# Scores of differential attention on the two row halves of the array

## The chip, the core and the metric

One NeuronCore of a Trainium2 chip runs the kernel. Its engines are TensorE (matrix products; its weight loads are a row of their own in the profile), VectorE, ScalarE, GpSimd, and SyncE, which issues the transfers. The metric is the device time of one execution in microseconds (us).

## The reference

One step of a streaming encoder with one layer: a prompt of 2048 frames of width 1024, and eight running streams that add 16 frames each to a past of 2048. Two attention branches run side by side (four differential heads, four latent-attention heads, MLA), each is gated, projected, and their gated sum is projected and added to the input. The change concerns the differential heads over the prompt:

```python
def diff_attention(q1, q2, q_pos, k1, k2, v, k_pos, lam):
    mask = chunk_mask(q_pos, k_pos)
    s1 = jnp.einsum('bqhd,bkhd->bhqk', q1, k1).astype(jnp.float32) * DIFF_SCALE
    s2 = jnp.einsum('bqhd,bkhd->bhqk', q2, k2).astype(jnp.float32) * DIFF_SCALE
    attn = masked_softmax(s1, mask) - lam * masked_softmax(s2, mask)
    return jnp.einsum('bhqk,bkhd->bqhd', attn.astype(v.dtype), v)
```

Queries and keys of either map ("lane") have 64 dimensions. The mask lets a query see keys up to the end of its own chunk of 64. Inputs and results are float32.

## The kernel before

Products run in a rounded float32 form that TensorE takes in one pass (F32R). To keep the accuracy of float32, an operand is split into a high part and a low part, and a product becomes several: high x high, high x low, low x high.

The kernel has stages: projections of the input (`_phase_a`), the latent heads' queries, keys and values (`_phase_a2`), the prompt's attention (`_phase_b`), the running streams' attention (`_sample`) and the output projections (`_phase_c`). The projections of the two output gates (`_gates`, tile z, products in `_mm3`, lines 98 to 100) are emitted with the lowest priority and fill gaps of TensorE in `_phase_b` and `_sample`. The order of instructions on each engine is set when the program is built, by a scheduler that takes the ready instruction with the highest priority, by a simulated time; priority follows the order of emission.

In `_phase_b` a differential and an MLA head step take turns. A step handles one group of 256 queries of one head (`attend`), as two tiles of 128 queries. For each tile `softmax` goes through the keys in chunks of 512 (the last one shorter). Per chunk and lane it takes a PSUM bank with tag "s" (four banks, shared by differential and MLA heads), fills it with the scores, takes the negated maximum on VectorE (line 977), the exponential with its sum on ScalarE (line 979), and the bank is free. Factors follow, then both lanes are combined, the result is transposed on TensorE (line 1032), split, and multiplied with the values (tile o, through `_mm3`).

The differential scores before: a lane's 64 rows of high parts and 64 rows of low parts of the keys lie in the 128 partitions, and the queries' tile holds the same 64 rows in both halves, once with the high part and once with the low part. So one product over 128 rows gives high x high + high x low, a second one low x high + low x low: two products for each lane (line 1078). The chunk on the diagonal gets the mask as one more product (line 1051), which adds -1e30 to 64 columns.

For comparison, later on: in `_sample` the scores of the running streams use parts of the array. Line 737 has four heads in four strips of 32 columns, line 819 strips of 64 columns over 128 rows, line 822 64 columns over 64 rows, line 780 strips of 32 columns over 16 rows. Their operands are plain float32, and TensorE makes two passes for each such product: a product is two entries of the profile.

Of the kernel before, what the change touches and what calls it, by code (L numbers as in the profile page):

```python
# [20 lines left out]
P = 128  # L21
D = 1024
SEQ = 2048
# [21 lines left out]
def _consts(c, pool):  # L45
# [17 lines left out]
    nc.gpsimd.memset(c.maskq[0:1, 0:64], 1.0)  # L63
    c.maskk = pool.tile([P, 64], BF16, name="maskk")
    nc.gpsimd.memset(c.maskk, 0.0)
    nc.gpsimd.memset(c.maskk[0:1, :], NEG)
# [37 lines left out]
def _rsqrt(c, out, ss, scale):  # L104
    # out = (ss * scale + EPS) ** -0.5, a few columns at a time
    n = ss.shape[1]
    c.nc.gpsimd.tensor_scalar(ss, ss, scale, EPS, op0=ALU.mult, op1=ALU.add)
    c.nc.gpsimd.tensor_tensor(out, ss, c.mhalf[:, :n], op=ALU.pow)
# [7 lines left out]
def _outer(c, stack):  # L116
    """Pools for the work that fills the engines' gaps: the projections of the gates, later the output projections."""
# [9 lines left out]
def _phase_a(c):  # L127
    nc, tc = c.nc, c.tc
    with (
# [141 lines left out]
        def first_units(us):  # L271
            # the factors of a group follow the sums of the next one
# [14 lines left out]
        def kpe_block():  # L287
            # 64 columns: the weights' two parts side by side, their products added after the load in the next phase
# [61 lines left out]
def _gates(c, prio, g, after, ready):  # L350
    """tanh(m / 2) of m_a and m_b for one group of tokens; ready: the parts of the weights come from memory."""
# [40 lines left out]
def _phase_a2(c):  # L392
    nc, tc = c.nc, c.tc
    with (
# [168 lines left out]
        # the factors of the next group lie between two parts of this one's products  # L563
# [15 lines left out]
def _lam(c, pool, psum):  # L579
    # every partition: exp(sum lq1 lk1) - exp(sum lq2 lk2) + lam_init, negated  # L580
# [12 lines left out]
def _sample_prep(c, temp, psum):  # L593
    """Rotated queries and keys of the new tokens, step by step: rows (s, d); the latent heads' queries in the latent space."""
# [56 lines left out]
    # both halves of the partitions: the streams of a pair take one each  # L651
# [19 lines left out]
def _sample(c, stack):  # L671
    """Attention of the running streams."""
# [25 lines left out]
    # row (h, s, q) of a batch belongs to column (h, q); the second map has weight -lam  # L698
# [9 lines left out]
    def softmax(scores, nm):  # L708
        # scores: PSUM views [128, n]; exponentials (two tiles of 1024 keys, the new keys) and their factors
# [9 lines left out]
        # pm holds the negated maxima  # L719
# [165 lines left out]
    # factors of the sub-norm of the prompt's heads and queries  # L885
# [22 lines left out]
def _phase_b(c):  # L908
    nc, tc = c.nc, c.tc
    GQ = 256  # L910
    with (
# [16 lines left out]
        def load_kv(name, src, shape):  # L928
            z = pkv.tile(shape, F32R, tag="kv", name=name)
            nc.sync.dma_start(z.bitcast(F32), src)  # L930
            return z

        class Chunks:
            """Keys [128, 512] or values [128, 4, 128] of one head, loaded 512 keys at a time."""

            def __init__(self, name, src, shape):
                self.name, self.src, self.shape, self.tiles = name, src, shape, {}

            def load(self, i):
                if i not in self.tiles:  # L940
                    n = self.shape[1]
                    self.tiles[i] = load_kv(f"{self.name}_{i}", self.src[:, i * n : (i + 1) * n], self.shape)

        def keys(name, src):
            return Chunks(name, src, [P, 512])

        def values(name, src):
            return Chunks(name, src, [P, 4, P])

        def load_q2(name, src, cols):  # L950
            # src [2 (hi, lo), 64, T]: both halves of the partitions get the same rows
# [9 lines left out]
        def softmax(diff, t, score, nm):  # L961
            """Exponentials of one tile of queries: per 512 keys ([per lane], first key, keys), and their factors."""
# [7 lines left out]
            for i, k0 in enumerate(starts):  # L970
                w = min(512, nk - k0)
                lanes = []
                for s in range(S):
                    ps = bank("s", f"s{nm}_{i}_{s}")
                    score(ps, s, k0, w, k0 + w == nk)
# [8 lines left out]
            # pm holds the negated maxima; per lane: factor of each piece over the sum  # L984
# [20 lines left out]
        def attend(diff, h, G, score, vh, vl, nm):  # L1005
            """O^T [dv, 256 queries] of one head in PSUM."""
# [6 lines left out]
            for i in range(2):  # L1013
                t = 2 * G + i
                es, a = softmax(diff, t, lambda ps, s, k0, w, last, t=t: score(ps, s, t, k0 // 512, w, last), f"{nm}_{i}")
# [347 lines left out]
```

## Time and profile before

| | |
|---|---|
| median of 3 runs | 2713.54 us (2703.49 to 2716.29) |
| span of the profiled execution | 2710.0 us |
| TensorE busy | 2569.4 us, 95% |
| VectorE, ScalarE, GpSimd busy | 1436.4, 1067.8, 703.5 us |
| bytes read from and written to memory | 351.55 and 141.66 MB |

The profile shows one execution: its own time is the span from the first to the last instruction, and the time of a run is measured apart from it. PE is TensorE's products, PEld its weight loads, which can overlap products; DVE is VectorE, ACT ScalarE, POOL GpSimd. Products are pipelined: the times of neighbours overlap, so that what one costs is read from start to start. In a shape, "64*128" ahead of the result's size is the part of the array that a product uses, rows by columns.

### The profile page before, as it was taken

To read this page: it belongs to the slowest core of one execution; us is meant where nothing else is said; L and a number is where in the kernel's file an instruction comes from. 1 tells how busy PE (TensorE), PEld (TensorE's weight loads), DVE (VectorE), ACT (ScalarE), POOL (GpSimd) and SP (SyncE) were. 2 spreads that over 40 slices of the span, in tenths; PEclk is the share of its full clock that TensorE was granted. 3 is DMA by queue.
4 is the path that set the end of the run, shared out by engine and by line. 5 is a ranking of instruction groups with operands and counts; after the bars stand their busy time and mean duration, and the time that the engine had idled before them with its cause. 6 is when DMAs were issued, how large, how long until landed. Compare 5 with 4: busy or idle time off the path is not lost. (4 is left out here: it accounts for less than half of the span.)

```text
span 2710.0 us, 44913 instructions
## 1 busy us (share of the span) xinstructions
PE 2569.4 (95%) x16308; PEld 2267.0 (84%) x16308; DVE 1436.4 (53%) x3038; ACT 1067.8 (39%) x2682; POOL 703.5 (26%) x944
## 2 busy tenths in 40 slices
PE   7999999999888889999999999999999999999998
PEld 7999999999778878988988888877566575888887
DVE  8236752233666467868776677892323222533334
ACT  5111223212343366766655666772323222311111
POOL 7102220001344233344333334442001001122211
PEclk9999999999889999999999999999999999999999
DMA  5346777322677873474565667317659576534332
GB/s 183 115 147 207 266 255 225 121 68 92 204 243 230 263 218 117 126 202 148 165 194 173 223 203 224 99 54 316 236 220 345 188 291 203 192 117 128 113 108 99
DMA packets 291372, 496.17 MB, mean 183 GB/s; under 512 B 27440, under 2 KB 229200, under 8 KB 280144
## 3 DMA queue, kind: packets, MB, share of 16 engines
q1 hardware_dynamic: 291152, 493.31, 55.5%
q8 instruction: 129, 2.11, 0.3%
q14 instruction: 91, 0.75, 0.1%
HBM read 351.55 MB, written 141.66 MB: 182 GB/s over the span
## 5 line engine op out<-in xcount | busy, mean ns | idle before, releaser
L98 PE MATMUL z<-z_hi,zw 128*128 128x384 f32 (+1 forms) x768 | 262.9, 342 | 26.2 <-ACT zt L388 21.1
L100 PE MATMUL z<-z_hi,zw 128*128 128x384 f32 (+1 forms) x768 | 256.3, 334 | 2.1 <-DMA zw<-wz 1.9
L99 PE MATMUL z<-z_lo,zw 128*128 128x384 f32 (+1 forms) x768 | 257.3, 335 | 0.6 <-POOL z_lo L370 0.6
L977 DVE TENSOR_REDUCE pmd<-sd 128x1 f32<-128x512 f32 (+3 forms) x320 | 189.7, 603 | 58.5 <-PE sd L1051 30.4
L979 ACT ACTIVATE ed<-sd,pmd 128x512 f32<-128x512 f32 (+3 forms) x320 | 200.6, 631 | 47.6 <-DVE pmd L977 35.6
L1078 PE MATMUL sd<-k,q 128*128 128x512 f32 (+2 forms) x640 | 191.0, 384 | 3.5 <-ACT ed L979 1.5
L1018 POOL TENSOR_SCALAR ed<-ed,ad 128x512 f32<-128x512 f32 (+3 forms) x160 | 117.0, 747 | 278.1 <-DVE ad L994 120.5
L98 PEld LDWEIGHTS z<-z_hi,zw 128*128 128x128 f32 x768 | 147.5, 192 | 44.6 <-ACT zt L388 25.4
L99 PEld LDWEIGHTS z<-z_lo,zw 128*128 128x128 f32 x768 | 147.7, 192 | 7.3 <-issue 4.7
L100 PEld LDWEIGHTS z<-z_hi,zw 128*128 128x128 f32 x768 | 146.9, 191 | 6.6 <-DMA zw<-wz 2.3
L1018 POOL TENSOR_SCALAR em<-em,am 128x512 f32<-128x512 f32 (+3 forms) x160 | 104.3, 668 | 157.2 <-DVE am L994 97.1
L98 PE MATMUL y<-o,wh_ab 128*128 128x384 f32 (+1 forms) x384 | 129.0, 336 | 14.9 <-DVE sm L1197 14.9
L113 DVE TENSOR_TENSOR zw<-zs,zw 128x512 fp32r<-128x512 f32 x128 | 89.9, 728 | 92.7 <-ACT zw L112 92.3
L370 POOL TENSOR_TENSOR z_lo<-zx,z_hi 128x384 fp32r<-128x384 f32 (+1 forms) x48 | 48.0, 1026 | 334.6 <-DVE gt L260 260.5
L98 PE MATMUL ps_u<-hi,wh_u 128*128 128x384 f32 (+1 forms) x384 | 126.0, 328 | 6.5 <-ACT wh_u L112 6.5
L100 PE MATMUL y<-o,wl_ab 128*128 128x384 f32 (+1 forms) x384 | 127.8, 333 | 1.4 <-DVE wl_ab L113 1.4
L99 PE MATMUL y<-o,wh_ab 128*128 128x384 f32 (+1 forms) x384 | 128.2, 334 | 0.4 <-DVE o L113 0.4
L1202 ACT ACTIVATE m<-sm 128x384 fp32r<-128x384 f32 (+1 forms) x48 | 24.4, 508 | 259.5 <-POOL sm L1200 259.5
L98 PE MATMUL ps_z<-hi,wh_z 128*128 128x384 f32 (+1 forms) x384 | 125.1, 326 | 1.0 <-ACT wh_z L112 1.0
L99 PE MATMUL ps_u<-lo,wh_u 128*128 128x384 f32 (+1 forms) x384 | 125.7, 327 | 0.0
L99 PE MATMUL ps_z<-lo,wh_z 128*128 128x384 f32 (+1 forms) x384 | 125.0, 325 | 0.0
L100 PE MATMUL ps_u<-hi,wl_u 128*128 128x384 f32 (+1 forms) x384 | 124.9, 327 | 0.0
(365 smaller groups left out, 7567.2 us busy)
## 6 DMA issues: line engine op xcount, KB each, us to landing
zs<-in_wu_dram SPq DMA_DIRECT2D x64, 512.0 KB
zw<-wz SPq DMA_DIRECT2D x64, 512.0 KB
ksd<-in_ckT_dram SPq DMA_DIRECT2D x32, 1024.0 KB
vsd<-in_cv_dram SPq DMA_DIRECT2D x32, 1024.0 KB
q<-Qs SPq DMA_DIRECT2D x128, 128.0 KB
ksm<-in_cc_dram SPq DMA_DIRECT2D x16, 1024.0 KB
smT<-zt SPq DMA_DIRECT2D x80, 192.0 KB
sm<-smT SPq DMA_DIRECT2D x80, 192.0 KB
```

The costliest lines, as they stand in the source:

```text
L98: nc.tensor.matmul(out, ah, bh, start=(j == 0), stop=False)
L99: nc.tensor.matmul(out, ah, bl, start=False, stop=False)
L100: last = nc.tensor.matmul(out, al, bh, start=False, stop=(j == n - 1))
L113: nc.vector.tensor_tensor(lo, src, hi.bitcast(F32), op=ALU.subtract)
L370: nc.gpsimd.tensor_tensor(lo[:, k], x[:, j], hi[:, k].bitcast(F32), op=ALU.subtract)
L977: nc.vector.tensor_reduce(nm_, ps[:, :w], axis=AX.X, op=ALU.max, negate=True)
L979: nc.scalar.activation(e[:, :w], ps[:, :w], AF.Exp, bias=nm_, accum_out=l[:, s, i : i + 1])
L1018: nc.gpsimd.tensor_scalar(p, p, a[:, 0, j : j + 1], 1.0, op0=ALU.mult, op1=ALU.mult)
L1078: nc.tensor.matmul(ps[:, :n], qs[s][:, j, qc], ks[s].tiles[i][:, :n], start=(j == 0), stop=(j == 1 and not last))
L1202: nc.scalar.mul(z[0], sm[0], 0.5)
```

## The change

Both lanes' queries lie in one tile: lane 0 in partitions 0 to 63, lane 1 in 64 to 127, with high and low part side by side. The keys' two tiles hold both lanes' high parts and both lanes' low parts. A score is now made of three products over 64 rows, without low x low, each lane on its own half of the array's rows, emitted in turn for both lanes. Both lanes' banks are taken ahead of the products. The mask has its row of ones in both halves. The MLA heads compute the same as before.

```diff
-    nc.gpsimd.memset(c.maskq[0:1, 0:64], 1.0)
+    for r in (0, 64):
+        nc.gpsimd.memset(c.maskq[r : r + 1, 0:64], 1.0)
...
-    nc.gpsimd.memset(c.maskk[0:1, :], NEG)
+    for r in (0, 64):
+        nc.gpsimd.memset(c.maskk[r : r + 1, :], NEG)
...
-        def load_kv(name, src, shape):
+        def load_kv(name, srcs, shape, at):
             z = pkv.tile(shape, F32R, tag="kv", name=name)
-            nc.sync.dma_start(z.bitcast(F32), src)
+            m = P // len(srcs)
+            for i, src in enumerate(srcs):
+                nc.sync.dma_start(z[i * m : (i + 1) * m].bitcast(F32), src[:, at])
             return z
 
+        def lane(scr, h, s):
+
+            return scr[h // 2].rearrange("l a (f j) t -> j l (a f) t", j=4)[(h % 2) * 2 + s]
...
-                for s in range(S):
-                    ps = bank("s", f"s{nm}_{i}_{s}")
-                    score(ps, s, k0, w, k0 + w == nk)
+                pss = [bank("s", f"s{nm}_{i}_{s}") for s in range(S)]
+                score(pss, k0, w, k0 + w == nk)
+                for s, ps in enumerate(pss):
                     nm_ = pm[:, s, i : i + 1]
                     nc.vector.tensor_reduce(nm_, ps[:, :w], axis=AX.X, op=ALU.max, negate=True)
...
-        def mask(ps):
-            nc.tensor.matmul(ps, c.maskq, c.maskk, start=False, stop=True)
+        def mask(ps, rows=slice(0, P)):
+            nc.tensor.matmul(ps, c.maskq[rows], c.maskk[rows], start=False, stop=True)
...
-            ks = []
-            for s in range(2):
-                src = c.Ks[h // 2].rearrange("l a (f j) t -> j (l a f) t", j=4)[(h % 2) * 2 + s]
-                ks.append(keys(f"k{h}_{s}", src[:, :SEQ]))
+
+            ks = [keys(f"k{h}_{l}", [lane(c.Ks, h, s)[l] for s in range(2)]) for l in range(2)]
...
-                qs = []
+                q = pq.tile([P, 2, GQ], F32R, tag="q", name=f"q{h}_{G}")
                 for s in range(2):
-                    src = c.Qs[h // 2].rearrange("l a (f j) t -> j l (a f) t", j=4)[(h % 2) * 2 + s]
-                    qs.append(load_q2(f"q{h}_{s}_{G}", src, cols))
+                    v = lane(c.Qs, h, s)[:, :, cols].rearrange("l p n -> p l n")
+                    nc.sync.dma_start(q[64 * s : 64 * s + 64].bitcast(F32), v)
...
-                def score(ps, s, t, i, w, last):
+                def score(pss, t, i, w, last):
                     qc = slice((t % 2) * P, (t % 2 + 1) * P)
                     n = max(w, 256)
-                    for j in range(2):
-                        nc.tensor.matmul(
-                            ps[:, :n], qs[s][:, j, qc], ks[s].tiles[i][:, :n], start=(j == 0), stop=(j == 1 and not last)
-                        )
+                    rows = [slice(64 * s, 64 * s + 64) for s in range(2)]
+                    for j, (lq, lk) in enumerate(((0, 0), (0, 1), (1, 0))):
+                        for r, ps in zip(rows, pss):
+                            nc.tensor.matmul(
+                                ps[:, :n], q[r, lq, qc], ks[lk].tiles[i][r, :n], start=(j == 0), stop=(j == 2 and not last)
+                            )
                     if last:
-                        mask(ps[:, w - 64 : w])
+                        for r, ps in zip(rows, pss):
+                            mask(ps[:, w - 64 : w], r)
```

## Rows read from the trace of the kernel before

**Rows 1.** The page's busy times: engine, us, share of the span, instructions.
```profile
PE 2569.4 (95%) x16308; PEld 2267.0 (84%) x16308; DVE 1436.4 (53%) x3038; ACT 1067.8 (39%) x2682; POOL 703.5 (26%) x944
```

**Rows 2.** Window of the prompt's attention: us, engines' busy us, clock, DMA share, GB/s.
```profile
942.00:1823.00 881.00, 856.55 (x5635) 756.41 (x5636) 668.44 (x1702) 577.88 (x1634) 344.67 (x532) 1.00 0.55 167
```

**Rows 3.** Groups by form, same stage: count, busy us, mean ns, idle before, releasers.
```profile
L1078 PE MATMUL sd<-k,q 128*128 128x512 f32 x448 | 147.1, 412 | 1.3 <-ACT ed L979 0.8 <-ACT em L979 0.5
...
L1078 PE MATMUL sd<-k,q 128*128 128x256 f32 x128 | 27.6, 299 | 1.8 <-issue 1.0 <-ACT ed L979 0.4 <-DMA k<-Ks 0.2
...
L1078 PE MATMUL sd<-k,q 128*128 128x384 f32 x64 | 17.4, 360 | 0.4 <-ACT ed L979 0.3
```

**Rows 4.** Timeline of TensorE's products: start us, us, engine, line, count.
```profile
1300.10 0.28 PE L99 MATMUL od<-ptld,v 128*128 128x256 f32 x1
1300.22 0.29 PE L100 MATMUL od<-pthd,v 128*128 128x256 f32 x1
...
1303.06 0.40 PE L1120 MATMUL sm<-kp,qp 128*128 128x512 f32 x1
1303.30 0.39 PE L1121 MATMUL sm<-kp,qp 128*128 128x512 f32 x1
1303.53 0.34 PE L1117 MATMUL sm<-kn,qn 128*128 128x384 f32 x1
1303.71 0.34 PE L1118 MATMUL sm<-kn,qn 128*128 128x384 f32 x1
1303.88 0.34 PE L1119 MATMUL sm<-kn,qn 128*128 128x384 f32 x1
```

**Rows 5.** Timeline where the used part changes, and line 822's weight loads' waits.
```profile
1992.36 0.44 PE L98 MATMUL z<-z_hi,zw 128*128 128x384 f32 x1
1992.64 0.33 PE L99 MATMUL z<-z_lo,zw 128*128 128x384 f32 x1
...
2001.79 0.33 PE L100 MATMUL z<-z_hi,zw 128*128 128x384 f32 x1
2002.05 1.07 PE L819 MATMUL ssm<-kTsm,sp 128*64 128x512 f32 x2
2003.05 1.07 PE L822 MATMUL ssm<-pesm,sp 64*64 64x512 f32 x2
2004.05 0.66 PE L809 MATMUL ktsm<-ident,ksm 128*128 128x128 f32 x4
...
  issue: 26.0, 32
```

**Rows 6.** Timeline of products in four column strips, from two windows.
```profile
1859.72 1.04 PE L737 MATMUL ssd<-ksd,sp 128*32 128x512 f32 x8
...
1860.15 1.04 PE L737 MATMUL ssd<-ksd,sp 128*32 128x512 f32 x8
```

**Rows 7.** Groups by form of ScalarE, same stage.
```profile
L979 ACT ACTIVATE ed<-sd,pmd 128x512 f32<-128x512 f32 x224 | 155.0, 695 | 39.1 <-DVE pmd L977 29.6 <-DVE ed L1025 2.3 <-DVE md L987 1.9
...
L979 ACT ACTIVATION_READ_ACCUMULATOR ed<-sd,pmd 128x1 f32 x320 | 65.6, 205 | 0.0
```

**Rows 8.** Timeline of the score products: first run, eight us, last run.
```profile
942.82 0.48 PE L1078 MATMUL sd<-k,q 128*128 128x256 f32 x2 [1.02 <-issue]
...
1353.06 0.71 PE L1078 MATMUL sd<-k,q 128*128 128x512 f32 x2
...
1354.19 0.40 PE L1078 MATMUL sd<-k,q 128*128 128x512 f32 x1
...
1354.45 0.94 PE L1078 MATMUL sd<-k,q 128*128 128x512 f32 x3
...
1359.46 0.63 PE L1078 MATMUL sd<-k,q 128*128 128x512 f32 x2
...
1818.83 0.71 PE L1078 MATMUL sd<-k,q 128*128 128x512 f32 x2
```

**Rows 9.** Waits of TensorE in the stage: us in total, times, longest.
```profile
PE sd L1078 <- DMA k<-Ks: 0.2, 1, 0.2
```

More of the change, by code (lines that the diff above doesn't have):

```diff
@@ L926, in _phase_b, with __init__ @@
         nc.sync.dma_start(kp.bitcast(F32), c.Kp.rearrange("l p t -> (l p) t")[:, :SEQ])
-        def load_kv(name, src, shape):
+        def load_kv(name, srcs, shape, at):
             z = pkv.tile(shape, F32R, tag="kv", name=name)
-            nc.sync.dma_start(z.bitcast(F32), src)
-            return z
+            m = P // len(srcs)
+            for i, src in enumerate(srcs):
+                nc.sync.dma_start(z[i * m : (i + 1) * m].bitcast(F32), src[:, at])
+            return z
+        def lane(scr, h, s):
+            return scr[h // 2].rearrange("l a (f j) t -> j l (a f) t", j=4)[(h % 2) * 2 + s]
         class Chunks:
-            def __init__(self, name, src, shape):
-                self.name, self.src, self.shape, self.tiles = name, src, shape, {}
+            def __init__(self, name, srcs, shape):
+                self.name, self.srcs, self.shape, self.tiles = name, srcs, shape, {}
             def load(self, i):
@@ L941, in load, with keys @@
                     n = self.shape[1]
-                    self.tiles[i] = load_kv(f"{self.name}_{i}", self.src[:, i * n : (i + 1) * n], self.shape)
-        def keys(name, src):
-            return Chunks(name, src, [P, 512])
+                    self.tiles[i] = load_kv(f"{self.name}_{i}", self.srcs, self.shape, slice(i * n, (i + 1) * n))
+        def keys(name, srcs):
+            return Chunks(name, srcs, [P, 512])
         def values(name, src):
-            return Chunks(name, src, [P, 4, P])
+            return Chunks(name, [src], [P, 4, P])
         def load_q2(name, src, cols):
@@ L1014, in attend @@
                 t = 2 * G + i
-                es, a = softmax(diff, t, lambda ps, s, k0, w, last, t=t: score(ps, s, t, k0 // 512, w, last), f"{nm}_{i}")
+                es, a = softmax(diff, t, lambda pss, k0, w, last, t=t: score(pss, t, k0 // 512, w, last), f"{nm}_{i}")
                 for j, (lanes, k0, w) in enumerate(es):
@@ L1099, in mla_head @@
         def mla_head(h, order):
-            kn = [keys(f"kn{h}_{i}", c.Kn[h, i]) for i in range(2)]
+            kn = [keys(f"kn{h}_{i}", [c.Kn[h, i]]) for i in range(2)]
             vh, vl = (values(f"vb{h}_{i}", c.Vb[i, h]) for i in range(2))
@@ L1109, in mla_head, with score @@
                         z.load(i)
-                def score(ps, s, t, i, w, last):
+                def score(pss, t, i, w, last):
+                    (ps,) = pss
                     qc = slice((t % 2) * P, (t % 2 + 1) * P)
```

## The prediction

> **What bounds the kernel now.** I read the page's busy times first: TensorE is busy for 95% of the span and no other engine for more than 53% [rows 1]. Then the windows by stage: the prompt's attention, the only stage that the edit touches, lies between 942 and 1823 us. There TensorE is busy 856.6 of 881 us at a granted clock of 1.00 (the 2.4 GHz level), VectorE 668, ScalarE 578, the DMA engines at 0.55 [rows 2]. So TensorE sets the pace of this stage too: it stands visibly idle for 24.4 us in all, and because its order of instructions is fixed at build time and gate projections (tile z) fill whatever the softmax leaves, time added to or taken from its products goes nearly whole into the end. Only the idle 24.4 us can absorb something.
>
> Third, what the touched products cost. The groups by form [rows 3] give the counts: 448 score products with 512 columns, 128 with 256, 64 with 384. Their mean times (412, 299, 360 ns) overlap one another, so the price of one is the step from start to start in the timeline [rows 4]: 0.235 us at 512 columns (1303.06, 1303.30, 1303.53), 0.175 at 384 (1303.53, 1303.71, 1303.88), 0.12 at 256 (1300.10 to 1300.22). The scores of both lanes now cost 448 x 0.235 + 128 x 0.12 + 64 x 0.175 = 105.3 + 15.4 + 11.2 = **131.9 us**.
>
> **Part 1, the products.** Per chunk of keys (160 chunks: 16 query tiles with one to four chunks, 40 a head) two products for each lane over all 128 rows become three for each lane over 64 rows: 640 become 960. A half-height product is not shorter: one of 64 rows and one of 128, both two passes over 512 columns, each take 1.00 us to the next start (2002.05, 2003.05, 2004.05) [rows 5]. So the price hangs on whether the two lanes' products run at once. The trace has no two products in different row halves side by side; the bounds are:
> - lanes one after the other: 960/640 x 131.9 = 197.8 us, **+65.9**;
> - lanes wholly at once: half of that, 98.9 us, **-33.0**.
> The nearest rows for "at once" are products in different column strips: the running streams' scores, four strips in turn, step on by 0.43 us per four passes over 512 columns (1859.72 to 1860.15) [rows 6], where one such pass by itself takes half of the 1.00 above. So the array does run neighbours together when they are issued back to back, and I take that for row halves too, but only where they are issued back to back.
>
> The Trainium skill, page "TensorEngine Tiling (Array Packing)", section "Theoretical Speedup", gives up to 2x for a dimension of 64 or less. By that alone the products would come to the -33.0 and the time to 2680, the third rival below; no run here shows it for row halves.
>
> They mostly won't be. The emitted order puts lane 1's first product right behind lane 0's, but each needs its own score bank, there are four (MLA shares them), and a bank comes free only when its exponential is through: 695 ns for one of 512 columns and 205 ns for reading its sum, on one engine [rows 7]. Banks thus come free at least 0.90 us apart, and three products of one lane take 0.70. When lane 0 has its bank and lane 1 hasn't, lane 0's other two products are ready and go first. The order of before shows this spacing: from 1353.06 on, runs of two score products of one lane stand between o or z products, with one joint run (1354.45) in six [rows 8]. Over the stage I count 299 such runs between the first (942.82) and the last (1818.83) [rows 8], and of the 160 chunks 111 have o or z products between their lanes and 49 nothing or only transposes. I take 111/160 = 0.69 apart and 0.31 at once: 0.69 x 197.8 + 0.31 x 98.9 = 167.2, that is **+35.3 us**.
>
> **Part 2, entering and leaving the halved array.** All other products of the stage use the whole array, so each run of score products now changes the array's shape twice. The trace prices such a change in the running streams [rows 5]:
> - waiting for what runs: a gate product of 384 columns is followed 0.26 us later by one on a 64-column strip (2001.79 to 2002.05) where its own step is 0.175: +0.09;
> - weights that can't be loaded ahead: on return to the whole array the first gate product needs 0.28 (1992.36 to 1992.64) where its step is 0.175: +0.105 for weights of 128 columns.
> The change of rows alone (128 to 64 rows, the same 64 columns, 2002.05 to 2003.05) costs the same as the others: two passes at 0.43 [rows 6] would be 0.86, the row says 1.00, so +0.14, with weights of half the width. And in all 32 visits of that form the weight load stood 0.81 us idle until the product before had ended (26.0 us in 32) [rows 5]. Price per change 0.09 + 0.105 = 0.195, per visit twice that, **0.39 us**. Bounds: 0 if halving only the rows at full width were free, which the 32 visits speak against; 0.39 if nothing is hidden. I take 0.39, since every change in these rows pays it. Number of visits: at least 160 (every chunk unbroken), 320 when all lanes stand apart, and some 28 more where a run is broken by transposes, as 1354.19 is now [rows 8]. I take 299, today's count: lanes that join and runs that break about cancel. 299 x 0.39 = **+116.6 us**.
>
> **Part 3, what costs nothing.** The masks stay 128 (four heads, 16 tiles, two lanes), now on 64 rows inside the visit. Queries: SP issues two loads per group in place of four; keys: two half-height loads per chunk in place of one. Together fewer issues on SP than now, and the score products wait 0.2 us for a key load in the whole stage [rows 9], so neither the smaller nor the halved loads can be seen; if that cover were gone it would be those tenths. Lane 0's maximum starts later, as its third product lies behind lane 1's second when they alternate: VectorE has 881 - 668 us free [rows 2], and TensorE has z products to fill with. The two added memsets run once, at the start, on GpSimd.
>
> **Sum.** +35.3 + 116.6 = +151.9 on TensorE. Its 24.4 us of visible waits [rows 2] I take as used up, since the engines that it waits for gain time when it is slower: **+127.5 us**. The profiled execution has a span of 2710.0; the median of the runs is 2713.5, 3.5 more, and I add the same: 2710.0 + 127.5 + 3.5 = **2841 us**.
>
> **Rivals.**
> - Lanes in turn, wholly at once. The two banks are there together, all 160 chunks are joint runs, 188 visits with broken ones: -33.0 + 188 x 0.39 = +40, less up to 24.4 of waits: 2730 to 2754. For it: 49 chunks behave so now. Against: the 0.90 us between banks.
> - Together in order, but not at once: +65.9 + 73.3 - 24.4 = +114.8, 2828; inside the forecast's range.
> - Not slower: changing only the rows at full width costs nothing and the pairs run at once: -33.0, so 2680. It decides as soon as a visit costs under 33/188 = 0.18 us with all lanes paired. For it speaks only that no row shows a change between the whole array and halves of full width; against it stand the 32 visits of [rows 5]. The Trainium skill's page "TensorEngine Tiling (Array Packing)", section "Key Properties", says that changing the tiling mode drains the engine; the trace agrees with 0.09 us a time.
> - No price for the change, but lanes apart: +35.3 to +65.9, less 24.4: 2724 to 2755.
>
> **How the numbers follow.** Lanes mostly apart with the price paid: 0.62, by itself 2803 (250 visits, half of the chunks joint: +16.5 + 97.5 - 24.4) to 2891 (348 visits, none joint: +65.9 + 135.7 - 24.4). Together and at once 0.18; together and serial 0.06; no price and apart 0.06; no price and paired 0.08. The range takes in the second and most of the fourth: 2728 to 2895. Half a per cent, 13.5 us, is about what a measurement of this kernel can tell (its three runs lie 12.8 apart). Faster by more than that: 0.08 (the last case). Within it: 0.04, the lower edges of the cases near 2727. Slower: 0.88.
>
> **What would show it.** Right: score products with 64 rows, whose runs begin with a step some 0.2 us over their plain one, with weight loads before them idle ("issue"), and the same again on the first product after a run; TensorE's sum over the stage up by 100 us or more, the stage longer by about as much, the stages before and after unchanged; the lanes' products of most chunks in separate runs, with starts 0.235 us apart, and only some starting within hundredths of each other. Wrong: runs of six with starts in pairs and a stage near its old length (first rival); plain steps at the ends of the runs (third and fourth); or a stage where TensorE waits for banks far more than 24 us, which would make the softmax the bound and none of these sums the right one.

## The result, and the profile after

The changed kernel takes **2911.56 us** (median; 2904.26 to 2914.64) against 2709.0 (2703.49 to 2716.29) for the kernel before in the same job: ratio 1.0738, 95% interval 1.0707 to 1.0769. The forecast said slower, 2841 us with a range of 2728 to 2895. The sign and the price of the edited stage held; the time lies above the range, because the stages behind grew too.

The page's busy times after the change, to be held against [rows 1]:

```profile
PE 2748.9 (94%) x16628; PEld 2329.5 (80%) x16628; DVE 1449.3 (50%) x3038; ACT 1080.0 (37%) x2682; POOL 697.4 (24%) x946
```

The span is 2910.3 us, 200.3 more than before; TensorE's busy time grew by 179.5. Now three windows of each kernel: the prompt's attention, cut from its first score product to its last value product; the running streams, up to the last stream's last value product (tile posd); the output. Columns: window, length, then busy us and count of each engine, granted clock, share of the DMA engines, GB/s. First the kernel before, with the attention cut a little later than in [rows 2]:

```profile
942.80:1843.30 900.50, 872.02 (x5729) 769.76 (x5730) 678.16 (x1725) 583.89 (x1649) 351.10 (x542) 0.99 0.54 164
1843.30:2302.20 458.90, 443.56 (x3331) 294.39 (x3330) 130.34 (x294) 143.18 (x372) 51.68 (x82) 0.99 0.70 265
2302.20:2710.00 407.80, 381.23 (x1957) 343.90 (x1954) 157.42 (x269) 78.78 (x172) 80.97 (x100) 0.98 0.39 126
```

The same windows of the changed kernel:

```profile
943.00:1984.10 1041.10, 1027.48 (x6048) 811.91 (x6048) 683.55 (x1717) 591.10 (x1643) 338.90 (x535) 0.99 0.43 131
1984.10:2468.40 484.30, 448.38 (x3284) 298.07 (x3283) 128.26 (x289) 142.10 (x368) 49.35 (x80) 0.95 0.64 243
2468.40:2910.30 441.90, 398.84 (x2002) 358.43 (x2002) 166.19 (x282) 85.34 (x184) 88.50 (x108) 0.95 0.41 133
```

The attention is 140.6 us longer, and that is work: TensorE is busy 155.5 us more. The forecast had +151.9 of work and +127.5 of time. The rest, 25.4 us in the running streams and 34.1 in the output, lies in stages that the edit doesn't touch. There the granted clock is 0.95 where it was 0.99 and 0.98, so TensorE spends more of them at the lower of its two levels (0.50, 1.2 GHz). Of the 25.4 us in the streams 20.6 are idle time of TensorE (35.9 in place of 15.3, length less busy).

**The visits.** A visit is a run of products on half the rows between products on the whole array. The timeline of the changed kernel at one visit, and at the mask that ends another (start us, length us, engine, line; "64*128" is half the array's rows):

```profile
1403.93 0.34 PE L100 MATMUL z<-z_hi,zw 128*128 128x384 f32 x1
1404.19 0.96 PE L1086 MATMUL sd<-k,q 64*128 64x512 f32 x3
1405.09 0.44 PE L101 MATMUL z<-z_lo,zw 128*128 128x384 f32 x1
1405.37 0.34 PE L102 MATMUL z<-z_hi,zw 128*128 128x384 f32 x1
...
1408.70 0.20 PE L1059 MATMUL sd<-maskk,maskq 64*128 64x64 bf16 x1
1408.83 0.45 PE L101 MATMUL z<-z_lo,zw 128*128 128x384 f32 x1
```

By the plain steps of [rows 4]: the gate product of 384 columns is followed after 0.26 in place of 0.175 (+0.085, the drain: waiting for what still runs); the three products take 0.90 in place of 3 x 0.235 = 0.705 (+0.195: a weight load that isn't hidden, and the drain on the way out); the first gate product afterwards takes 0.28 (+0.105, the other weight load). Together +0.385, the 0.39 of the forecast. The other visits agree: the median step in is 0.269 over the 66 visits behind a product of 384 columns, three products of 512 columns take 0.890, and the first product of 384 columns behind a visit takes 0.281 (48 visits). Where a transpose follows (101 visits), its step is 0.165 in place of 0.109, so only 0.056 more. A mask at the end changes little: it leaves after 0.13, where a full-height mask in the kernel before left after 0.04, and that 0.09 is the drain again. The view of line 1086 shows its weight loads held back, about once for every two or three visits ("issue": us, times):

```profile
L1086 PEld LDWEIGHTS sd<-k,q x960: 182/184/334, 943.0 to 1957.6; 64*128 64x128 f32 x192
...
  issue: 29.3, 148
```

In the starts of all products I count 345 visits, masks included (before: 299 such runs), and 85 of the 480 pairs of one lane's product with the other's that start within 30 ns of each other, mostly 3 to 10 ns. The Trainium skill, page "TensorE: Matmul & The Clock Gate", section "The mechanism", gives about 4 ns between the starts of products in different row groups. The traces agree where the pairs are issued in turn (in e6 below, 290 of 341 start 3 or 4 ns apart); here the gap is often 10 ns or more.

**The stages behind.** The timeline at the end of the changed kernel's attention; brackets give idle time ahead and what ended it:

```profile
1980.03 0.28 PE L102 MATMUL z<-z_hi,zw 128*128 128x256 f32 x1
1981.25 0.59 PE L1101 MATMUL od<-sqd,ones 128*1 128x256 f32 x2 [0.94 <-DVE ogd L1100]
1982.88 0.38 PE L100 MATMUL om<-pthm,vb 128*128 128x256 f32 x1 [1.04 <-ACT ssd L1103]
...
1983.69 0.42 PE L102 MATMUL om<-pthm,vb 128*128 128x256 f32 x1
1991.16 0.31 PE L745 MATMUL snsd<-sp 128*32 128x16 f32 x8 [7.05 <-DMA sp<-sp]
1995.98 0.69 PE L100 MATMUL z<-z_hi,zw 128*128 128x384 f32 x1 [4.51 <-ACT zw L114]
...
1999.43 0.53 PE L101 MATMUL z<-z_lo,zw 128*128 128x384 f32 x1
1999.75 0.53 PE L102 MATMUL z<-z_hi,zw 128*128 128x384 f32 x1
```

The last filler of the attention (tile z) stands at 1980.03, 3.7 us ahead of the last value product; in the kernel before it stands at 1670.01, 173 us ahead. Behind it there is nothing to cover the running streams' preparation: TensorE waits 7.05 us for the new tokens' load (tile sp, issued at the attention's end in both kernels) and 4.51 for the next gate group's weights. That group is late: the last two loads of its inputs (tile zx) go out at 1983.4 and 1985.6, in the kernel before at 1676.0 and 1677.1. There, 46 gate products of the next group stand ahead of the same snsd product (scores of the streams' new keys), the first of them 0.13 us after the last value product. From 1983.4 on the granted clock is 0.50, the level of 1.2 GHz, for 17.1 us, and gate products step on by 0.32 in place of 0.175:

```profile
1983.40:2000.50 17.10, 5.54 (x26) 4.91 (x26) 4.32 (x9) 3.55 (x8) 9.62 (x18) 0.50 0.84 304
```

There is a second such place in the streams. The late group lasts to 2232.6, and the first product of the last group comes at 2258.4; in between TensorE waits 4.93 us for a factor (tile Wsd) and 6.83 for gate weights, the longer of the two waits of this row (us in total, times, longest):

```profile
PE z L100 <- ACT zw L114: 11.3, 2, 6.8
```

With this, three more stretches in the streams are at the lower level: 13.7 us from 2010.7 on, 13.7 from 2236.0 and 6.8 from 2256.5. The kernel before has 6.8 us of it in all of its streams. At the end of the streams, 17 gate products come behind the last stream here, and no product of the output projection (tile y) ahead of it, where the kernel before has 0 and 31. TensorE's waits in the first 92 us of the output, changed kernel (us in total, times, longest):

```profile
PE y L100 <- ACT o L114: 9.4, 2, 5.1
PE y L100 <- ACT wh_ab L114: 7.8, 1, 7.8
```

and again a stretch at the lower clock level, 23.9 us from 2478.3 on:

```profile
2478.30:2502.20 23.90, 10.53 (x27) 7.79 (x28) 13.34 (x16) 10.92 (x15) 2.98 (x4) 0.50 0.86 297
```

### The profile page after: what moved, and what is told of

Same layout as the page of the kernel before. It is cut to its first block, busy times and chain, and to the rows that moved or that the text cites. A ratio compares the mean times of both kernels' runs of the same rounds, so it can differ in the third digit from the quotient of the medians.

```text
span 2910.3 us, 45460 instructions
## 1 busy us (share of the span) xinstructions
PE 2748.9 (94%) x16628; PEld 2329.5 (80%) x16628; DVE 1449.3 (50%) x3038; ACT 1080.0 (37%) x2682; POOL 697.4 (24%) x946
## 5 line engine op out<-in xcount | busy, mean ns | idle before, releaser
L100 PE MATMUL z<-z_hi,zw 128*128 128x384 f32 (+1 forms) x768 | 269.5, 351 | 32.6 <-ACT zt L390 18.1
L1086 PE MATMUL sd<-k,q 64*128 64x512 f32 (+2 forms) x960 | 269.3, 405 | 1.3 <-ACT ed L987 1.3
L102 PE MATMUL z<-z_hi,zw 128*128 128x384 f32 (+1 forms) x768 | 261.7, 341 | 0.2 <-DVE zw L115 0.2
L1026 POOL TENSOR_SCALAR ed<-ed,ad 128x512 f32<-128x512 f32 (+3 forms) x160 | 109.9, 702 | 389.8 <-DVE ad L1002 178.4
L1086 PEld LDWEIGHTS sd<-k,q 64*128 64x128 f32 x960 | 137.7, 186 | 66.4 <-issue 29.3
L1043 ACT CAST pthd<-ptd 128x512 fp32r<-128x512 f32 (+3 forms) x160 | 82.7, 522 | 134.9 <-PE ptd L1040 134.4
L1044 DVE TENSOR_TENSOR ptld<-ptd,pthd 128x512 fp32r<-128x512 f32 (+3 forms) x160 | 96.0, 604 | 58.4 <-ACT pthd L1043 57.8
```

Source lines behind the costliest of these rows:

```text
L100: nc.tensor.matmul(out, ah, bh, start=(j == 0), stop=False)
L102: last = nc.tensor.matmul(out, al, bh, start=False, stop=(j == n - 1))
L1026: nc.gpsimd.tensor_scalar(p, p, a[:, 0, j : j + 1], 1.0, op0=ALU.mult, op1=ALU.mult)
L1043: nc.scalar.copy(hi, v)
L1044: nc.vector.tensor_tensor(ptl[ch][:, :n, i * P : (i + 1) * P], v, hi.bitcast(F32), op=ALU.subtract)
L1086: nc.tensor.matmul(ps[:, :n], q[r, lq, qc], ks[lk].tiles[i][r, :n], start=(j == 0), stop=(j == 2 and not last))
```

## The experiments

Two questions: does a visit to half the rows cost what the sum says (theory "shape"), and where do the 60 us behind the attention come from? Stage lengths below are cut as above; where a run has a control, the control carries the verdict. The kernel before ran beside each on the same chip: its medians are 2716.2 us beside e1 to e4, 2711.8 beside e5 to e9, 2712.1 beside e10 to e12, 2716.3 beside e13 and e14.

### The products without the halves

`e1_full_rows`: three products a lane, over all 128 rows, the other lane's half of the query tile set to zero.

```diff
-                q = pq.tile([P, 2, GQ], F32R, tag="q", ...)        # one for both lanes
+                q = pq.tile([P, 2, GQ], F32R, tag="q", ...)        # one per lane
                 nc.sync.dma_start(q[64 * s : 64 * s + 64].bitcast(F32), v)
+                nc.gpsimd.memset(q[64 - 64 * s : 128 - 64 * s].bitcast(F32), 0.0)
...
-                                ps[:, :n], q[r, lq, qc], ks[lk].tiles[i][r, :n], ...
+                                ps[:, :n], q[:, lq, qc], ks[lk].tiles[i][:, :n], ...
```

> Three products a lane as in the change, emitted in turn with both banks taken first, but each over all 128 rows: every lane has its own query tile with zeros in the other lane's half, so no product uses half of the array. 960 products in sequence are 197.8 us where the kernel before has 131.9. Theory 'shape' (entering and leaving the halved array costs about 0.39 us a run): +66 less up to 24 of TensorE's waits, 2750 to 2776 us, and the running streams' stage as long as before. Theory 'products' (the third product and the lanes' order cost, the halves themselves nothing): as slow as the change, 2880 to 2915. Theory 'order' (the new order moves gate products and waits into the running streams' stage, some 60 us): that stage stays about 540 us long here as well, total 2810 or more.

Measured: 2769.67 us, ratio 1.0200 (1.0179 to 1.0221). Its attention window:

```profile
938.60:1891.90 953.30, 931.68 (x6049) 825.31 (x6050) 687.03 (x1724) 588.47 (x1650) 373.03 (x604) 0.99 0.48 145
```

TensorE's work is up by 59.7 us: 320 more full-height products cost 0.187 each (the forecast had +65.9). The products alone are 2% of the time, inside the range of "shape"; the other 95.8 us of the changed kernel's +155.5 come with the half height, and are net of what its pairs save. The streams and the output take 464.3 and 412.0 us here, near their old lengths.

### The shape without the products

`e2_mask_half`: the kernel before, its masks (192 of them, MLA's included) on 64 rows; they have one row of ones, so the values are the same.

```diff
-            nc.tensor.matmul(ps, c.maskq, c.maskk, start=False, stop=True)
+            nc.tensor.matmul(ps, c.maskq[0:64], c.maskk[0:64], start=False, stop=True)
```

> The kernel before, with its 192 mask products (128 of them on differential scores) on 64 rows in place of 128; the other 64 rows held zeros, so the result is the same, and the order of the products is the same. Each mask is then alone in the halved array, between products of the whole one. 'Shape': 192 x 0.3 to 0.39 = +58 to +75 us on TensorE, less up to 24 of waits: 2743 to 2784. 'Products' and 'order': nothing changes, 2695 to 2723.

Measured: 2744.19 us, ratio 1.0103 (1.0081 to 1.0126). The order is unchanged, the attention's work is up by 38.0 us:

```profile
937.80:1870.40 932.60, 910.01 (x5729) 785.72 (x5730) 678.66 (x1725) 586.40 (x1650) 349.36 (x541) 0.99 0.52 158
```

That is 0.20 us for each of 192 visits of a 64-column product. The time lies at the low edge of its range, but the price of 0.3 to 0.39 did not come: it is half to two thirds of it. The timelines say why. First the half-height mask, then the full one in the kernel before:

```profile
1300.39 0.39 PE L1078 MATMUL sd<-k,q 128*128 128x256 f32 x2
1300.71 0.20 PE L1051 MATMUL sd<-maskk,maskq 64*128 64x64 bf16 x1
1300.84 0.39 PE L98 MATMUL od<-pthd,v 128*128 128x256 f32 x1
```

```profile
1301.04 0.40 PE L1078 MATMUL sd<-k,q 128*128 128x256 f32 x2
1301.28 0.20 PE L1051 MATMUL sd<-maskk,maskq 128*128 128x64 bf16 x1
1301.32 0.42 PE L99 MATMUL z<-z_lo,zw 128*128 128x384 f32 x1
1301.57 0.34 PE L100 MATMUL z<-z_hi,zw 128*128 128x384 f32 x1
```

The kernel before already paid after a mask: its next product steps on by 0.25 in place of 0.175. So most of the 0.105 of the way out is not new there. A weight load of 128 columns takes 0.19 us in the trace and the mask's own step is 0.04; that the load behind so short a product can't be hidden is the likely reason, argued only.

### Both lanes forced together: two-bank tiles

`e3_pair_banks`: the changed kernel, both lanes' scores in one tile of two banks, so that one wait frees both. `e4_pair_banks_before`: the same tile for the kernel before, as its control.

```diff
-                pss = [bank("s", f"s{nm}_{i}_{s}") for s in range(S)]
+                if diff or i % 2 == 0:
+                    two = pp.tile([P, 2, 512], F32, tag="s", name=f"s{nm}_{i}", bufs=2)
+                pss = [two[:, 0], two[:, 1]] if diff else [two[:, i % 2]]
```

> The change, with both lanes' scores in one PSUM tile of two banks (two such tiles; an MLA head puts two chunks in one), so that both lanes' banks come free together. The order then has 154 runs of score products in place of 345, most of them all six products of a chunk. 'Shape', with row halves that run at once: -33 + 154 x 0.39 = +27 us against the kernel before, 2712 to 2750. 'Shape', with halves that run one after the other: +66 + 60, 2811 to 2840. 'Products': 2880 or more. 'Order': the running streams' stage stays long, 2770 or more.

> Control for the tiles of two banks: the kernel before with its two products a lane over 128 rows, and the same tiles of two banks as the run beside it. No product changes. All theories: 2695 to 2750; what it takes more than the kernel before is the price of fewer, larger bank tiles, and is to be taken off the run with the halved array.

Measured: 2872.84 us, ratio 1.0587 (1.0564 to 1.0610), and 3017.38, ratio 1.1114 (1.1095 to 1.1134). Both missed, by the same mechanism: the attention windows, e3 and then its control,

```profile
938.20:1996.60 1058.40, 938.81 (x6050) 777.90 (x6050) 709.84 (x1725) 595.55 (x1651) 353.18 (x542) 0.94 0.44 132
```

```profile
946.70:2144.20 1197.50, 997.28 (x5729) 824.56 (x5730) 712.42 (x1725) 588.18 (x1648) 346.34 (x542) 0.90 0.41 123
```

show TensorE idle for 119.6 and 200.2 us (length less busy), with a lower granted clock: four banks used in twos starve it. Against its control the attention with the changed scores is 139 us shorter here. That doesn't speak for them where TensorE is the bound; that a shorter chain from bank to bank is what wins is argued, not shown.

### Both lanes forced together: chains and blocks, one bank each

`e5_lane_by_lane` swaps the loops (lane 0's three products, then lane 1's); `e6_chain` keeps the order of the change and chains the six products; `e8_one_block` issues the six and their masks as one block; `e9_one_block_before` does so with the products of the kernel before, as its control.

```diff
 # e5
-                    for j, (lq, lk) in enumerate(((0, 0), (0, 1), (1, 0))):
-                        for r, ps in zip(rows, pss):
+                    for r, ps in zip(rows, pss):
+                        for j, (lq, lk) in enumerate(((0, 0), (0, 1), (1, 0))):
 # e6
+                            with tc.issue_after(mm.ins) if mm else nullcontext():
+                                mm = nc.tensor.matmul(...)
 # e8, and e9 in the kernel before
+                    with tc.tile_critical():
```

> The changed kernel with the loops swapped: lane 0's three half-height products, then lane 1's, so nothing is next to the other half to run at once. The prompt attention: products serial +65.9 us, 305 runs at the forecast's 0.39 us = +119 (or at 0.31 us, which is what the changed kernel's stage leaves per run), less some 15 us of waits: 145 to 170 us longer than before. The order on TensorE that comes out has no gate product left for the end and 36 of the output projection's products ahead of the last of the running streams, as before's has 0 and 31. Theory 'order' (the changed kernel's 60 us behind the attention come from its own fixed order of gate products, not from halved products): the running streams near 460 and the output near 410 us, in all 2850 to 2885 us. Rival 'halves' (the 60 us belong to the halved products wherever they stand): these stages stay some 60 us longer, 2905 to 2940 us.

> The changed kernel with its six products per chunk chained in the written order (lane 0, lane 1, lane 0, ...), each lane keeping its own one-bank tile: 301 runs, some 130 of them a single product of lane 0 that stands ahead of a run of five. In a run of five two pairs can go at once and one product stands alone, so a chunk takes four product times in place of three when everything pairs: products about 126 us, 6 less than before's 131.9. Theory 'shape' (a visit to the half-height array costs 0.31 to 0.39 us): +93 to +117 us for the visits, less some 15 to 25 us of waits: attention 65 to 95 us longer, in all 2780 to 2810 us. Rival 'products' (what counts is whether lanes pair, the visits are cheap): pairs are there, so at or below before, 2690 to 2720 us. Order of the later stages as in before: they stay near 460 and 410 us.

> The changed kernel with the six products of a chunk and its masks issued as one block (nothing else of TensorE between them), each lane in its own one-bank tile: 150 runs and every pair at once. Products -33.0 us. Theory 'shape': visits 150 x 0.31 to 0.39 = +47 to +59 us, so TensorE's work 14 to 26 us above that of the control that blocks before's products in the same way; in all the control's time plus 14 to 26 us. Rival 'products' (visits cheap once the lanes pair): 33 us below the control, and at or below the kernel before if the block costs nothing in waits. What the block costs in waits for two free banks the control shows.

> Control: before's two full-height products of both lanes and their masks issued as one block per chunk in the same way (150 runs). Products and shapes as before; only the block's waits for two free banks are new: 0 to 40 us, in all 2705 to 2755 us. If it is far above that, a block of both lanes starves TensorE by itself, as the two-bank tiles did.

Measured: e5 2838.33 us, ratio 1.0462 (1.0444 to 1.0479); e6 2790.57, ratio 1.0284 (1.0263 to 1.0304); e8 3057.24, ratio 1.1269 (1.1253 to 1.1286); e9 3094.44, ratio 1.1414 (1.1392 to 1.1436).

e5, all three windows:

```profile
942.30:1967.30 1025.00, 1005.24 (x6049) 804.39 (x6050) 687.83 (x1724) 590.28 (x1648) 345.98 (x541) 0.99 0.45 136
1967.30:2431.60 464.30, 450.86 (x3336) 298.81 (x3334) 129.90 (x295) 142.88 (x372) 51.01 (x82) 0.99 0.70 263
2431.60:2841.00 409.40, 380.60 (x1949) 343.45 (x1949) 156.81 (x268) 78.99 (x172) 79.39 (x99) 0.98 0.40 125
```

With 305 visits and the same halved products the stages behind are back at 464 and 409 us: they don't belong to the halves. The total is 12 us under its range. One expectation in it was wrong: lane 0's last and lane 1's first product do lie side by side, and 130 pairs start together.

e6, its attention window, then one of its visits:

```profile
936.60:1910.20 973.60, 954.09 (x6050) 769.38 (x6050) 687.43 (x1725) 585.52 (x1651) 348.18 (x543) 0.99 0.48 143
```

```profile
1402.98 0.96 PE L1088 MATMUL sd<-k,q 64*128 64x512 f32 x5
1403.87 0.39 PE L102 MATMUL od<-pthd,v 128*128 128x256 f32 x1
```

Five products take 0.89 us (1402.98 to 1403.87), as long as the three of the changed kernel above (0.90): the pairs do run at once. 341 pairs start together, and TensorE still works 82.1 us more than before, with 301 visits. Price per visit, worked out in three kernels with the forecast's step (serial +65.9, less 131.9/640 = 0.206 for each pair that starts together):

| kernel | work added | pairs at once | products | visits | us per visit |
|---|---|---|---|---|---|
| changed | 155.5 | 85 | +48.4 | 345 | 0.31 |
| e5 | 133.2 | 130 | +39.1 | 305 | 0.31 |
| e6 | 82.1 | 341 | -4.3 | 301 | 0.29 |

With e1's measured +59.7 as the serial bound, and so 0.20 for a pair, the three prices are 0.33, 0.33 and 0.30. "Shape" explains all three with one price, and e6 lies in its range. The rival "products" (cheap visits, pairing decides) had e6 at 2720 or less, 70 us under what it took.

e8 fell outside its theory: 37 us below its control, where 14 to 26 above was expected, and near the rival's 33. The windows of the two (e8, then e9):

```profile
950.40:2185.40 1235.00, 981.21 (x6049) 811.38 (x6050) 668.94 (x1725) 587.64 (x1648) 341.94 (x542) 0.88 0.37 111
```

```profile
948.40:2220.80 1272.40, 1010.23 (x5730) 830.54 (x5731) 666.66 (x1725) 584.36 (x1648) 339.21 (x542) 0.90 0.38 114
```

One block of 512 columns of each (e8, then e9; in brackets the idle time ahead):

```profile
1510.58 0.96 PE L1087 MATMUL sd<-k,q 64*128 64x512 f32 x6 [0.44 <-POOL ed L1026]
```

```profile
1502.72 1.20 PE L1080 MATMUL sd<-k,q 128*128 128x512 f32 x4 [0.44 <-ACT zt L388]
```

In both, TensorE is idle for over 250 us of the stage, and it stood idle ahead of each of the 150 blocks and behind 139 and 141 of them (in the changed kernel ahead of 2 and behind 2 of 345 visits). So what it costs to enter and leave falls into waits that are there anyway, and these two don't price a visit as the real kernel pays it. What is left to see is the blocks themselves: all 480 pairs start together in e8, and a block takes 0.964 us in place of 1.200 (medians at 512 columns), less by the step of one product, 0.235. Over all chunks (112 x 0.235 + 16 x 0.175 + 32 x 0.12) that is 33.0 us, the forecast's bound for lanes wholly at once; TensorE's busy time differs by 29.0. That the waits hide the price is read from the starts; no run took the waits away.

### What makes the stages behind longer

A gate group is 16 units of 24 products. `e10_gate_late`: the kernel before, its last gate unit tied behind the last stream. `e11_gates_early`: the changed kernel, the last gate group's products planned at the early priority that their loads have; `e12_before_gates_early` is the same in the kernel before.

```diff
 # e10, kernel before
+        if g == 4 and u == 15:
+            after = c.po.ins          # the last value product of the last stream
 # e11, and e12 in the kernel before
-        with tc.issue_after(after) if after else nullcontext():
+        with tc.issue_after(after) if after else nullcontext(), ahead() if g == 4 else nullcontext():
```

> The kernel before with one edge added to the order: the last unit of gate products (24 products) waits for the last value product of the last running stream, as 17 of the changed kernel's do. The prompt attention's order and products stay before's. Theory 'order' (the 60 us of the changed kernel behind the attention come from where its gate products ended up): attention unchanged at 900, the output 25 to 40 us longer than before's 408 (the output projection's first products now stand behind this unit and wait), the running streams little changed, since the other units stay in place; in all 2735 to 2760 us. Rival 'halves': the late unit costs its own moved work only, 2705 to 2720 us.

> The changed kernel with the products of the last group of gates planned at the early priority that their preparation has: TensorE's order is the same up to the end of the prompt attention (345 runs), and behind it no gate product is left for after the last running stream; 36 of the output projection's products stand ahead of it. Theory 'order': attention 1041 us as in the changed kernel, running streams back to 460-468 and output to 408-415, in all 2845 to 2865 us. Rival 'halves': 2900 to 2915 us, unchanged.

> Control: the kernel before with the same early priority for the last group of gates. Its order has no late gate product to repair, so by theory 'order' there is nothing to win: 2700 to 2725 us, within 0.5% of before. If it gains some 50 us as well, the early priority is worth that to any order, and the changed kernel's order was not what cost it.

Measured: e10 2736.38 us, ratio 1.0095 (1.0080 to 1.0110); e11 2907.96, ratio 1.0728 (1.0711 to 1.0746); e12 2744.30, ratio 1.0110 (1.0083 to 1.0136). e10's output, then e11's streams and output, then e12's streams:

```profile
2295.80:2739.90 444.10, 400.78 (x2011) 360.74 (x2009) 166.09 (x282) 85.24 (x184) 88.29 (x108) 0.94 0.42 132
```

```profile
1980.10:2497.50 517.40, 468.88 (x3336) 319.68 (x3335) 136.82 (x303) 148.47 (x380) 58.26 (x89) 0.92 0.65 242
2497.50:2903.00 405.50, 380.41 (x1953) 343.33 (x1949) 156.99 (x268) 78.81 (x172) 79.75 (x99) 0.98 0.40 126
```

```profile
1850.50:2336.00 485.50, 463.02 (x3336) 308.98 (x3334) 130.63 (x295) 143.16 (x372) 53.08 (x82) 0.96 0.68 251
```

e10 came out as expected and puts the changed kernel's output into the kernel before: 444.1 us (changed: 441.9), nearly the same busy time and clock. One late unit of fillers costs 36 us there. e11 takes it out: 405.5. But the streams went the other way, to 517.4, and the total stayed; the control e12 also lost 26.6 us in its streams. That the early priority used up the filler that the streams need is the likely reason, argued only. So e10 prices the late unit in the output, and both leave the 25 us of the streams open. The expectation that 2845 to 2865 would come out was wrong, as was e12's.

`e13_filler_ends_early` goes to the place of the first wait: the last four units of the last group that fills the attention (group 5) get the early priority. `e14_before_filler_early` is its control.

```diff
-        with tc.issue_after(after) if after else nullcontext():
+        with tc.issue_after(after) if after else nullcontext(), ahead() if g == 5 and u >= 12 else nullcontext():
```

> The changed kernel with the last four units of the gate group that fills the prompt attention planned at the early priority, so that the last of them stands 236 products ahead of the attention's last one in place of 7; 342 runs in place of 345; behind the attention TensorE's order is the kernel before's (46 gate products ahead of the first running stream's new-key scores, none left for the end). Theory 'filler': the 60 us come from the filler lasting to the very end of the attention, so that the next group's factors and weights are late, the running streams start without cover, and the units slip into the output. Then the attention stays at 1035 to 1045 us, the running streams come back to 458-466 and the output to 408-412, in all 2840 to 2860 us. Rival 'halves': the stages behind stay 60 us longer whatever the order, 2900 to 2915 us.

> Control: the kernel before with the same early priority for the same four units. Its filler already ends 1052 products ahead of the attention's last; the stages behind keep their order, so by theory 'filler' nothing is won: 2700 to 2725 us. If it gains as much as the changed kernel does, the early priority is worth that to any order.

Measured: e13 **2860.29 us**, ratio 1.0529 (1.0512 to 1.0545); e14 2715.39, ratio 0.9997 (0.9982 to 1.0012). e13's three windows:

```profile
941.40:1986.60 1045.20, 1028.52 (x6050) 813.33 (x6050) 689.69 (x1725) 593.84 (x1651) 346.11 (x543) 0.99 0.45 133
1986.60:2448.90 462.30, 448.57 (x3335) 296.72 (x3334) 129.74 (x295) 142.78 (x372) 51.57 (x82) 0.99 0.70 264
2448.90:2857.90 409.00, 382.13 (x1949) 344.92 (x1949) 156.23 (x268) 78.89 (x172) 79.50 (x99) 0.98 0.40 125
```

The attention does the same work (1028.5 us busy, 342 visits), its last filler now ends 44 us ahead of the last value product, and the streams and the output are back at 462.3 and 409.0 us. The same edit gives the kernel before nothing. The last two zx loads of the next group go out at 1945.3 and 1947.0, again ahead of the attention's end (last value product at 1986.3). So the 55 us (926.2 to 871.3 for both stages) come with the order and not with the halves: with a filler that lasts to the very end of the attention and a next group that is late behind it. Of the streams' 25.4 us, 20.6 are idle time; how much of the rest is the clock, these runs don't separate.

## Why the prediction was right, and where it failed

**What bounds the kernel.** Right. TensorE's work in the stage grew by 155.5 us and the stage by 140.6; waits took up 14.9 us of it (28.5 idle before, 13.6 after), where the forecast let them take all of its 24.4.

**Products: +35.3 forecast, +48.4 worked out.** The two bounds held: pairs run wholly at once when issued side by side (e6, e8), and in turn otherwise. The share was mis-sized: 0.31 expected, 85 of 480, or 0.18, found. (The forecast's 167.2 comes to 167.1 by its own terms, which changes nothing.) The reason given, that each lane waits for its own bank and the other lane's products go first, is what the order shows: 126 of the 345 visits are three products, 62 more three and a mask, and only 18 hold six, with or without masks. e1 puts the serial bound at +59.7 in place of +65.9.

**Visits: 299 x 0.39 = +116.6 forecast, 345 x 0.31 = +107.1 found.** Each step of a visit measured what [rows 5] said (0.085 to 0.105 each, four a visit). Two sizes were off against each other, which is luck. There are more visits, because runs that break outweigh lanes that join: 50 of the 345 are a single product and 43 are two, a lane's three broken up, and 11 are a mask alone. And the net price is lower, because the kernel before wasn't at plain steps: after a mask it paid 0.075, and 79 of its 326 steps from score to score (all 79 at 512 columns) already took 0.30 us or more in place of 0.235. About 128 x 0.075 + 79 x 0.085 = 16 of the 27 us between the two prices are that, and some 5 are the 101 visits followed by a transpose (0.056 in place of 0.105); the rest isn't assigned.

**The step that failed: "the stages before and after unchanged".** The stage before was unchanged (the attention starts at 942.8 and 943.0 us). The stages after took 59.5 us more, and this alone puts the time out of the range: 2911.6 less 59.5 is 2852, 11 from the forecast, and e13, the same kernel with that repaired, took 2860. That it comes so near is in part luck: against the forecast the products are 13.1 us more, the visits 9.5 less and the waits taken up 9.5 less. In place of "unchanged" the runs show this: the gate products that fill the attention ended 3.7 us ahead of its end in place of 173, the next group's loads went out late, TensorE stood uncovered at two places of the streams, and 17 gate products slipped behind them into the output; e13, which ends that filler earlier, gives 55 us of the 59.5 back. How the edit got there is argued, not run: it changes how long the score products take in the scheduler's simulated time, and with that where the low-priority fillers come to lie in the whole order. The forecast counted the fillers as cover and never asked where they would run out. Why this particular order stretched them so far wasn't tried: e1 leaves 19 us between the last filler and the end, e5 53, e6 81, the changed kernel 3.7, and of these only the last one lost time behind it.

**The rivals.** "Together and at once" needed all chunks joint, and that did not come. It would not have beaten the kernel before either, by an estimate from the table: 188 visits at 0.29 cost 55 us, and all pairs at once save 33.0. The two rivals without a price for the change are out: four steps per visit are in the timeline. Without a wait in front, a block of six at 512 columns takes 0.894 us (median, e6), one of four full-height products 1.009 in the kernel before: pairing gains 0.115, while drain and weight load outside the block cost 0.19. No version of the change beat the kernel before.

## What to carry to other kernels

Using part of the array was paid for by the visit here, not by the product: count how often the order enters and leaves it, price one visit from a place where the shape already changes, and subtract what the old order paid at the same spot. An order that fills gaps with low-priority work is one object: after any edit that changes durations, look where the filler ends, since a filler that lasted to the end of the stage left the next one without cover here. And a comparison made where TensorE waits anyway (the banks in twos, the blocks) doesn't give the price that holds where it hardly ever waits.

## What the runs showed that I had not expected

- Taking banks in twos, or both lanes as one block, costs the kernel before about 300 and 380 us by itself (3017 and 3094 us): TensorE idles 200 to 262 us of the stage, and the granted clock averages 0.90 in it.
- One unit of 24 gate products at the wrong place costs 36 us in the output of the profiled run (e10; 24 us in the medians), though its own work is 24 x 0.175 = 4.2 us. Behind it TensorE waits 17 us. Around the same waits of the changed kernel the lower clock level holds for 23.9 us with 10.5 us of products in it, which by an estimate would be half as long at the upper level.
- The kernel before ran its own products less smoothly than a plain pitch suggests: 79 of its 233 steps from one score product of 512 columns to the next take 0.30 us or more, not 0.235. Pricing a new cost against ideal steps overstates it.
